# A hybrid decoder block: layer norms on VectorE alone in one row, the output projection's trailing products first, and a first chunk loaded and split by contraction tile

## The chip, the cores and the metric

The kernel runs on one core of a Trainium2 chip. The metric is the device time of one execution, in microseconds (us): three runs gave 1086.43, 1087.6 and 1087.9, median 1087.6. A separate execution was recorded by the hardware profiler; its rows are used below.

## The reference

One decoder layer on x of 256 tokens by 2048 features, all in float32:

```
proj = x @ w_in                        # 2048 x 6160, cut into conv gates b, c, u, and q, k, v, r, z
y_conv = group_rms_norm(b * causal_dwconv3(c * u))
y_gla  = group_rms_norm(gated linear attention of q, k, v, decay from z) * silu(r)
mix = concat(y_conv, y_gla) @ w_out    # 2048 x 2048
x = layer_norm(alpha * x + mix) * ln1_g + ln1_b
ff = square(relu(x @ w_ff_up)) @ w_ff_down   # 2048 x 8192, 8192 x 2048
x = layer_norm(alpha * x + ff) * ln2_g + ln2_b
```

Layer norm here is: mean and variance over the 2048 features of a token, subtract the mean, divide by the square root of variance plus 1e-5, multiply by a gain and add a bias per feature.

## The kernel before

**Tiles.** The 256 tokens are two tiles (t = 0 and t = 1) of 128 partitions. A matrix product runs over the contraction in tiles of 128; two of them (KC = 2) make a *chunk* of weights, 128 partitions by 2 by up to 512 columns. The weights stream once from HBM in chunks, through a pool of 13 raw buffers.

**Three products for one.** Every float32 operand is split into a high part (rounded to the matmul's input type) and a low part, the rest: `split` (L109 to L111) copies the high part on ScalarE (L110) and subtracts on VectorE (L111). `products` (L145) then does three matmuls per contraction tile: high by high (L155), high by low (L156), low by high (L157). So one chunk for one token tile is six matmuls of 512 columns, and each chunk costs one ScalarE copy and one VectorE subtraction of 128 x 1024.

**Who orders the work.** A list scheduler orders the instructions of each engine when the kernel is built: by program order where several are ready, by its own estimate of when they are ready. `tc.issue_after(ins)` sets one instruction behind another in the issue order of the same engine; it adds no wait. `queued(on, ...)` (L100) chains what it emits on one engine in this way while `queue` has a key for that engine: during the first block of the input projection for "pe", "act", "dve" and "sync".

**Lagged products.** `Lagged` (L162) runs a chunk's product for t = 0 at once and puts the one for t = 1 off by `lag` chunks. Each product is a step; `soon` is a list of [count, function]: after each step every count goes down by one, and at zero the function is emitted, with `issue_after` the step's last matmul. Split weights wait in 9 slots (5 "hl" and 4 "s8") from the split to the product for t = 1. In the output projection the lag is 5, so after the last product for t = 0 five products for t = 1 remain (the *trailing products*).

**Layer norm 1.** When all four 512-column blocks of a token tile have been added up (`done_mix`, L610: residual add L613, block statistics L614), `layer_norm` (L575) merges the statistics (L578), `inv_sqrt` (L223) takes the square root on ScalarE (L226), and five VectorE instructions of one element per partition follow (L228 to L233: reciprocal and one Newton step). Then each block is *centred* (subtract the mean, times the gain, L586 on VectorE) and *scaled* (times the inverse deviation, plus the bias, L595 on VectorE). `LN1_HOW = "dppp"` does the centring of the last three blocks in two steps, on ScalarE (L589) and GpSimd (L590). A finished block is transposed on TensorE into x1T by `put` (L218: four transposes into one of two PSUM banks; then L110 and L111 split the result): at once for t = 0, and after 1 + `X1_WAIT` steps for t = 1.

**Up projection.** `up_first` (L662) starts the feed-forward part: chunk for chunk of w_ff_up against x1T, with the trailing products of the output projection run in turn with it, as the lag (`LAGS`: 5, then 8 for two chunks, then 5) lets them go. Each block of x1T feeds two chunks. Later groups mix the up and down projections; there VectorE also forms sums of weight chunks.

**Layer norm 2** comes at the end, in the same function, once per token tile: all on VectorE for t = 0; `LN2_HOW = "qddp"` for t = 1 (first block: centre and scale on ScalarE and GpSimd; fourth block: centre on both). Each block is stored as it is done.

**Start.** The first block of the input projection (412 columns) loads its chunk 0 of weights (`raw_p`, 412 KB) and of the transposed input (`xr`, 256 KB, `x_ahead`, L262) as one DMA each on SP's queue, weights first, splits the weights, then the input.

Of the kernel before, what the change touches and what calls it, by code (L numbers as in the profile page):

```python
# [18 lines left out]
P = 128  # L19
# [23 lines left out]
LAGS = [LAG] * LAG + [LAG + 3] * 2 + [LAG]  # L43
RING = 4096
LN1_HOW = "dppp"
LN2_HOW = "qddp"
X1_WAIT = [2, 4, 6, 8]
# [4 lines left out]
WAIT_UP = 6  # L52
BEHIND = 6
# [8 lines left out]
def hymba_block(ctx, tc, x, x_t, w_in, conv_w, conv_g, w_gate, gate_b, gla_g, w_out,  # L62
# [53 lines left out]

    homes = [[(hlp, "hl")], 0]
# [20 lines left out]
    def weight_chunks(w, kts, at, ncol, name):  # L138


        for i in range(0, len(kts), KC):
            raw = raw_chunk(w, kts[i], at, ncol, f"{name}_{i}")
            yield kts[i:i + KC], *parts_of(raw, ncol, f"{name}_{i}")
# [46 lines left out]
    def project(lagged, w, kts, at, ncol, lhs, done, name, ps=None, first=True, last=True,  # L190
                before=None, lags=None):

        ps = {} if ps is None else ps
        n = len(kts) // KC
        for i, chunk in enumerate(weight_chunks(w, kts, at, ncol, name)):
            if before is not None:
                before(i)

            if lags is not None:
                lagged.lag = lags[i]  # L200
# [22 lines left out]
    def inv_sqrt(pool, ms, eps_t, eps, n, name):  # L223
# [4 lines left out]
        nc.vector.reciprocal(r, s)  # L228
        q = pool.tile([P, n], F32, tag=f"is_q{n}", name=f"q_{name}")
        nc.vector.tensor_mul(q, r, r)  # L230
        nc.vector.scalar_tensor_tensor(q, ms, eps, q, op0=ALU.add, op1=ALU.mult)
        nc.vector.tensor_scalar(q, q, -0.5, 1.5, op0=ALU.mult, op1=ALU.add)
        nc.vector.tensor_mul(r, r, q)  # L233
        return r

# [17 lines left out]
    with ExitStack() as p1:  # L253
# [8 lines left out]
        def x_ahead(i):  # L262
# [3 lines left out]
            split(xT[half][0][:, j:j + KC, :], xT[half][1][:, j:j + KC, :], raw)  # L266

# [63 lines left out]
        block(*qkvz(0), before=x_ahead)  # L331
# [218 lines left out]
    with ExitStack() as p2:  # L550
# [24 lines left out]
        def layer_norm(t, stats, gt, bt, name, done, how="dddd"):  # L575
            y = ys[t]
            mv = sm2.tile([P, 2], F32, tag="mv", name=f"mv_{name}_{t}")
            nc.vector.bn_aggr(mv, stats)  # L578
            rstd = inv_sqrt(sm2, mv[:, 1:2], eps_ln, LN_EPS, 1, f"{name}_{t}")
            shift = sm2.tile([P, 1], F32, tag="shift", name=f"shift_{name}_{t}")  # L580
            if how != "dddd":
                nc.scalar.mul(shift, mv[:, 0:1], -1.0)
            for b, way in enumerate(how):
                cols = slice(b * D // len(how), (b + 1) * D // len(how))
                if way == "d":
                    nc.vector.scalar_tensor_tensor(y[:, cols], y[:, cols], mv[:, 0:1], gt(cols),  # L586
                                                   op0=ALU.subtract, op1=ALU.mult)
                else:
                    nc.scalar.activation(y[:, cols], y[:, cols], AF.Identity, bias=shift)  # L589
                    nc.gpsimd.tensor_mul(y[:, cols], y[:, cols], gt(cols))  # L590
                if way == "q":
                    nc.scalar.activation(y[:, cols], y[:, cols], AF.Copy, scale=rstd)
                    nc.gpsimd.tensor_add(y[:, cols], y[:, cols], bt(cols))
                else:
                    nc.vector.scalar_tensor_tensor(y[:, cols], y[:, cols], rstd, bt(cols),  # L595
                                                   op0=ALU.mult, op1=ALU.add)
                done(b, cols)

# [11 lines left out]
        def done_mix(t, ps, nb):  # L610
# [5 lines left out]
            if left[t] == 0:  # L616
                def done(b, cols):
# [7 lines left out]
                    if t == 0:  # L625
                        go()
                    else:
                        lag.soon.append([1 + X1_WAIT[b], go])
                layer_norm(t, stats1[t], g1, b1, "ln1", done, how=LN1_HOW)

# [31 lines left out]
        def up_first(hT):  # L662

            for i in range(GROUP // NB):
                def done(t, ps, i=i):
                    r = ht.tile([P, NB], F32, tag="relu", name=f"relu_0_{i}_{t}")
                    hidden(r, ps, hT, i, t, f"h0_{i}_{t}", 1 + WAIT_H)
                if i == 1:
                    homes[:] = [[(hlp, "hl")], 0]
                    lag.lag = 0  # L670
                project(lag, w_up, list(range(KT)), i * NB, NB, x1lhs, done, f"up0_{i}",
                        lags=LAGS if i == 0 else None, before=sums_ahead if i == 1 else None)
# [134 lines left out]
        def add(g, t, ps, c0, n):  # L807
# [9 lines left out]
            if left2[t] == 0:  # L817
                def store(b, cols):
                    queue_of = nc.scalar if LN2_HOW[b] == "q" else nc.sync
                    queue_of.dma_start(out[t * P:(t + 1) * P, cols], y[:, cols])  # L820
                layer_norm(t, stats2[t], *gb2, "ln2", store, how=LN2_HOW if t == NT - 1 else "dddd")
# [46 lines left out]

        hTs = [t8_pair("hT_0")]
# [75 lines left out]
```

## Time and profile before

| what | value |
|---|---|
| runs (median of 3) | 1086.43, 1087.6, 1087.9 (1087.6) us |
| the profiled execution's own time | 1086.87 us |
| its span, first to last instruction | 1085.1 us |
| mean granted TensorE clock (1 is 2.4 GHz) | 0.995 |
| busy: TensorE matmul, VectorE, ScalarE, GpSimd | 98%, 82%, 55%, 1% |
| HBM traffic | 201 GB/s over the span |

The profiled execution took 1.77 us more than its span, and lies 0.73 us under the median of the runs. PE is the matmul side of TensorE, PEld its weight loads, DVE is VectorE, ACT ScalarE, POOL GpSimd, SP the queue that issues most DMAs. A matmul's recorded duration overlaps the next one's, so the spacing of starts is what a matmul costs; VectorE's instructions overlap a little in the same way.

### The profile page before, as it was taken

The numbers are of one execution on the slowest core, as the hardware profiler recorded it, in microseconds if no ns is written. First come the engines' busy times: TensorE is split into PE (matmuls) and PEld (weight loads), VectorE is DVE, ScalarE is ACT, GpSimd is POOL, SyncE is SP. The second block draws the span as 40 slices with busy tenths as digits, with TensorE's granted clock in tenths as the row PEclk, the third lists the DMA queues.
The fourth block names the chain that finished last, engine by engine and source line by source line (L and its number), as shares of the span: only waits on it lengthen the run. The fifth ranks groups of instructions, "written<-read, shape, count | busy, mean of one in ns | idle before, by whom it ended". The sixth has DMA issues, their size and how long they took to land.

```text
span 1085.1 us, 13282 instructions
## 1 busy us (share of the span) xinstructions
PE 1062.4 (98%) x4914; PEld 892.2 (82%) x4914; DVE 888.8 (82%) x1003; ACT 594.0 (55%) x685; POOL 15.4 (1%) x18
## 2 busy tenths in 40 slices
PE   9999999999999979999999999999999999999994
PEld 8998888888888868788888888888888888888884
DVE  6545558567656687999999999999999999999667
ACT  6475554435643535666556556556556656556431
POOL 0000000000000020000000000000000000000001
PEclk9999999999999999999999999999999999999997
DMA  9976358676676644257566567567567467368712
GB/s 342 314 245 212 99 180 275 200 232 212 197 294 194 195 174 136 80 205 256 175 211 217 177 209 235 163 203 236 162 201 257 135 207 259 130 203 263 240 57 78
DMA packets 68678, 218.69 MB, mean 202 GB/s; under 512 B 7107, under 2 KB 17363, under 8 KB 68358
## 3 DMA queue, kind: packets, MB, share of 16 engines
q1 hardware_dynamic: 65024, 207.78, 58.2%
q10 hardware_dynamic: 3590, 10.08, 2.7%
q8 instruction: 38, 0.62, 0.2%
q14 instruction: 26, 0.21, 0.1%
HBM read 214.67 MB, written 3.15 MB: 201 GB/s over the span
## 4 chain that ended last, share of the span: by engine, by line
PE 91%; DVE 6%; ACT 1%; DMA 1%; issue 1%; DVEq 0%
PE ps_dn L156 10%; PE ps_dn L157 10%; PE ps_dn L155 10%; PE ps_p L157 3%; PE ps_p L156 3%; PE ps_p L155 3%; PE ps_o L157 2%; PE ps_o L156 2%; PE ps_o L155 2%; PE ps_upa L155 2%; PE ps_upc L155 2%; PE ps_upa L157 2%; PE ps_upa L156 2%; PE ps_upc L156 2%; PE ps_upc L157 2%; PE ps_upd L155 2%
## 5 line engine op out<-in xcount | busy, mean ns | idle before, releaser
L110 ACT CAST hl_up<-raw_r 128x1024 fp32r<-128x1024 f32 x196 | 206.4, 1054 | 129.8 <-PE ps_dn L157 65.7
L111 DVE TENSOR_TENSOR hl_up<-raw_r,hl_up 128x1024 fp32r<-128x1024 f32 x196 | 236.8, 1218 | 9.8 <-ACT hl_up L110 9.3
L110 ACT CAST hl_dn<-raw_dn 128x1024 fp32r<-128x1024 f32 x128 | 134.9, 1054 | 123.6 <-PE ps_dn L157 104.7
L155 PE MATMUL ps_dn<-hl_dn,hT_hi 128*128 128x512 f32 x496 | 193.5, 391 | 0.0
L157 PE MATMUL ps_dn<-hl_dn,hT_lo 128*128 128x512 f32 x496 | 193.1, 389 | 0.0
L156 PE MATMUL ps_dn<-hl_dn,hT_hi 128*128 128x512 f32 x496 | 193.0, 389 | 0.0
L111 DVE TENSOR_TENSOR hl_dn<-raw_dn,hl_dn 128x1024 fp32r<-128x1024 f32 x128 | 156.0, 1219 | 22.5 <-ACT hl_dn L110 21.6
L157 PEld LDWEIGHTS ps_dn<-hl_dn,hT_lo 128*128 128x128 f32 x496 | 93.1, 188 | 19.6
L155 PEld LDWEIGHTS ps_dn<-hl_dn,hT_hi 128*128 128x128 f32 x496 | 93.1, 188 | 19.2
L156 PEld LDWEIGHTS ps_dn<-hl_dn,hT_hi 128*128 128x128 f32 x496 | 93.1, 188 | 19.1
L111 DVE TENSOR_TENSOR hl_p<-raw_p,hl_p 128x824 fp32r<-128x824 f32 (+1 forms) x40 | 40.3, 1017 | 33.1 <-ACT hl_p L110 31.4
L111 DVE TENSOR_TENSOR hl_o<-raw_o,hl_o 128x1024 fp32r<-128x1024 f32 x32 | 38.8, 1223 | 32.8 <-ACT hl_o L110 32.5
L110 ACT CAST hl_o<-raw_o 128x1024 fp32r<-128x1024 f32 x32 | 33.4, 1055 | 45.2 <-PE ps_o L157 38.5
L155 PE MATMUL ps_p<-hl_p,xT_hi 128*128 128x412 f32 (+1 forms) x160 | 56.1, 351 | 0.3 <-ACT xT_hi L110 0.3
L157 PE MATMUL ps_p<-hl_p,xT_lo 128*128 128x412 f32 (+1 forms) x160 | 56.1, 351 | 0.1
L156 PE MATMUL ps_p<-hl_p,xT_hi 128*128 128x412 f32 (+1 forms) x160 | 56.1, 350 | 0.0
L110 ACT CAST hl_p<-raw_p 128x824 fp32r<-128x824 f32 (+1 forms) x40 | 35.1, 885 | 26.9 <-PE ps_p L157 21.3
L155 PE MATMUL ps_upa<-hl_up,x1T_hi 128*128 128x512 f32 x112 | 45.1, 403 | 0.0
L155 PE MATMUL ps_upc<-hl_up,sum_s 128*128 128x512 f32 x112 | 44.3, 396 | 0.0
L157 PE MATMUL ps_upa<-hl_up,x1T_lo 128*128 128x512 f32 x112 | 43.7, 390 | 0.0
L156 PE MATMUL ps_upa<-hl_up,x1T_hi 128*128 128x512 f32 x112 | 43.7, 390 | 0.0
L156 PE MATMUL ps_upc<-hl_up,sum_s 128*128 128x512 f32 x112 | 43.7, 390 | 0.0
(279 smaller groups left out, 2154.6 us busy)
## 6 DMA issues: line engine op xcount, KB each, us to landing
raw_dn<-in_w_ff_down_dram SPq DMA_DIRECT2D x128, 512.0 KB, 4.2
raw_r<-in_w_ff_up_dram SPq DMA_DIRECT2D x112, 512.0 KB, 3.6
raw_o<-in_w_out_dram SPq DMA_DIRECT2D x32, 512.0 KB, 3.5
raw_p<-in_w_in_dram SPq DMA_DIRECT2D x24, 412.0 KB, 5.4
raw_c<-in_w_in_dram SPq DMA_DIRECT2D x16, 512.0 KB, 4.2
raw_u<-in_w_in_dram SPq DMA_DIRECT2D x16, 512.0 KB, 4.3
raw_b<-in_w_in_dram SPq DMA_DIRECT2D x16, 512.0 KB, 4.2
raw_r<-in_w_in_dram SPq DMA_DIRECT2D x16, 512.0 KB, 3.5
```

Source lines behind the costliest of these rows:

```text
L110: queued("act", lambda: nc.scalar.copy(hi, src))
L111: queued("dve", lambda: nc.vector.tensor_sub(lo, src, hi.bitcast(F32)))
L155: nc.tensor.matmul(ps[:, :ncol], ah, whi[:, j, cols], start=f, stop=False, skip_group_check=more)
L156: nc.tensor.matmul(ps[:, :ncol], ah, wlo[:, j, cols], start=False, stop=False, skip_group_check=more)
L157: nc.tensor.matmul(ps[:, :ncol], al, whi[:, j, cols], start=False, stop=e, skip_group_check=more)
```

## The change

1. `layer_norm` does every block on VectorE. Its instructions are chained by `issue_after` in one order: the first block's centring (while ScalarE takes the root), the five small instructions, the first block's scaling, then centre and scale of the second, third and fourth block in turn. ScalarE and GpSimd no longer take part, in layer norm 1 and 2.
2. After the second block's scaling a mark is left in `held`: once `LN1_BUT` (3 for t = 0, 6 for t = 1) more weight chunks have been split, the VectorE part of all later splits is set behind that instruction.
3. `lag.flush()` before `up_first` emits the five trailing products ahead of the up projection. The lag in the first half of the up group is 6 throughout. Both token tiles' transposes now go through `soon`, with waits [6, 7, 9, 11] and [5, 7, 8, 9] steps.
4. The first chunk (`begin`) is loaded and split contraction tile by contraction tile: input half, weight half, input half, weight half, as four DMAs, with a ScalarE copy and a VectorE subtraction for each half. The order within a half is input first.
5. Layer norm 2 stores its blocks on SP's and ScalarE's queue in turn.

```diff
-LAGS = [LAG] * LAG + [LAG + 3] * 2 + [LAG]
+LAG_UP = 6
-LN1_HOW = "dppp"
-LN2_HOW = "qddp"
-X1_WAIT = [2, 4, 6, 8]
+X1_WAIT = [[6, 7, 9, 11], [5, 7, 8, 9]]
+LN1_BUT = [3, 6]
...
     def parts_of(raw, ncol, name):
...
-        split(hl[:, 0, :, :ncol], hl[:, 1, :, :ncol], raw)
+        behind = None
+        for h in held:
+            behind = h[1] if h[0] <= 0 else behind
+            h[0] -= 1
+        with nullcontext() if behind is None else tc.issue_after(behind):
+            split(hl[:, 0, :, :ncol], hl[:, 1, :, :ncol], raw)
...
+    def in_row(steps):
+
+        for i, step in enumerate(steps):
+            with tc.issue_after(nc.cur_bb.bb.instructions[-1]) if i else nullcontext():
+                step()
...
+        def begin(at, ncol):
+
+            raw = rawp.tile([P, KC, NB], F32, tag="raw", name="raw_begin")
+            hl = hlp.tile([P, 2, KC, NB], F32R, tag="hl", name="hl_begin")
+            src = piece(w_in, 0, at, ncol)
+            for j in range(KC):
+                load(xr[0][:, j, :], x_t[0][:, j, :])
+                load(raw[:, j, :ncol], src[:, j, :])
+                split(xT[0][0][:, j, :], xT[0][1][:, j, :], xr[0][:, j, :])
+                split(hl[:, 0, j, :ncol], hl[:, 1, j, :ncol], raw[:, j, :ncol])
+            return hl[:, 0], hl[:, 1]
...
-        block(*qkvz(0), before=x_ahead)
+        at, ncol, done, name = qkvz(0)
+        block(at, ncol, done, name, before=lambda i: i and x_ahead(i), begun=begin(at, ncol))
...
-        def layer_norm(t, stats, gt, bt, name, done, how="dddd"):
+        def layer_norm(t, stats, gt, bt, name, done, but):
...
+            def centre(cols):
+                nc.vector.scalar_tensor_tensor(y[:, cols], y[:, cols], mv[:, 0:1], gt(cols),
+                                               op0=ALU.subtract, op1=ALU.mult)
+
+            rstd = inv_sqrt(sm2, mv[:, 1:2], eps_ln, LN_EPS, 1, f"{name}_{t}",
+                            meanwhile=lambda: centre(blocks[0]))
+            queue["dve"] = nc.cur_bb.bb.instructions[-1]
+            for b, cols in enumerate(blocks):
+                if b:
+                    queued("dve", lambda: centre(cols))
+                queued("dve", lambda: nc.vector.scalar_tensor_tensor(y[:, cols], y[:, cols], rstd, bt(cols),
+                                                                     op0=ALU.mult, op1=ALU.add))
+                if b == 1:
+                    held.append([but, queue["dve"]])
                 done(b, cols)
+            del queue["dve"]
...
-                    if t == 0:
-                        go()
-                    else:
-                        lag.soon.append([1 + X1_WAIT[b], go])
+                    lag.soon.append([X1_WAIT[t][b], go])
...
+                lag.lag = LAG_UP if i == 0 else 0
...
-                    queue_of = nc.scalar if LN2_HOW[b] == "q" else nc.sync
+                    queue_of = nc.scalar if b % 2 else nc.sync
...
+        lag.flush()
         hTs = [t8_pair("hT_0")]
         up_first(hTs[0])
```

## Rows read from the trace of the kernel before

**Rows 1.** The page's first lines: the span, and each engine's busy time, share of the span and instructions.

```profile
span 1085.1 us, 13282 instructions
PE 1062.4 (98%) x4914; PEld 892.2 (82%) x4914; DVE 888.8 (82%) x1003; ACT 594.0 (55%) x685; POOL 15.4 (1%) x18
```

**Rows 2.** The view of waits, of TensorE's matmul side in the stretch from 360 to 430 us: what waited, for whom, us in total, times, longest.

```profile
PE pt_x L218 <- DVE y L595: 2.8, 1, 2.8
PE pt_x L218 <- issue: 1.7, 1, 1.7
PE pt_x L218 <- DVE x1T_lo L111: 0.8, 1, 0.8
PE ps_up L157 <- DVE x1T_lo L111: 0.7, 1, 0.7
```

**Rows 3.** Busy time by stretch: the stretch and its length, then us busy (and instructions) of PE, PEld, DVE, ACT, POOL, then TensorE's granted clock, the DMA engines' busy share and GB/s.

```profile
402.00:410.00 8.00, 8.00 (x44) 6.64 (x44) 3.07 (x5) 1.98 (x4) 0.00 (x0) 1.00 0.28 113
...
520.00:600.00 80.00, 80.00 (x362) 66.20 (x361) 77.90 (x77) 47.33 (x49) 0.00 (x0) 1.00 0.64 210
...
1071.00:1085.00 14.00, 0.08 (x1) 0.00 (x0) 10.56 (x17) 2.44 (x5) 4.27 (x3) 0.59 0.40 150
```

**Rows 4.** Timeline of PE around layer norm 1: start, duration, line, operation, in brackets the idle time before it and what ended it. The first row starts the output projection's product of the last block, third chunk, for t = 1; the second that of the eighth and last chunk.

```profile
372.42 0.39 PE L155 MATMUL ps_o<-hl_o,mixT_conv_hi 128*128 128x512 f32 x1
...
379.22 0.39 PE L155 MATMUL ps_o<-hl_o,mixT_gla_hi 128*128 128x512 f32 x1
382.43 1.32 PE L218 MATMUL pt_x<-ident,y 128*128 128x128 f32 x8 [2.82 <-DVE y L595]
...
401.25 0.50 PE L157 MATMUL ps_up<-hl_up,x1T_lo 128*128 128x512 f32 x1 [0.69 <-DVE x1T_lo L111]
```

**Rows 5.** One piece of the chain of work that ended last, a `put` on PE: start, length.

```profile
402.44 0.44 PE pt_x L218 x4
```

**Rows 6.** Timeline of VectorE around layer norm 1. L613 is the residual add of the last block of t = 0, L614 its statistics, L578 the merge; L231 and L233 are two of the five small instructions; the two last rows are of t = 1.

```profile
373.49 0.68 DVE L613 SCALAR_TENSOR_TENSOR y<-y,ps_o 128x512 f32<-128x512 f32 x1
374.21 0.69 DVE L614 BATCH_NORM_STATS2 st<-y 128x6 f32<-128x512 f32 x1
374.94 0.26 DVE L578 BATCH_NORM_AGGREGATE mv_ln<-st 128x2 f32<-128x24 f32 x1
...
378.14 1.25 DVE L231 SCALAR_TENSOR_TENSOR q_ln<-mv_ln,q_ln 128x1 f32<-128x1 f32 x1
...
379.62 1.00 DVE L233 TENSOR_TENSOR r_ln<-r_ln,q_ln 128x1 f32<-128x1 f32 x1
380.66 3.71 DVE L595 SCALAR_TENSOR_TENSOR y<-y,r_ln,b_ln 128x512 f32<-128x512 f32 x4
...
385.42 1.27 DVE L111 TENSOR_TENSOR x1T_lo<-pt_x,x1T_hi 128x512 fp32r<-128x512 f32 x2
...
393.62 1.21 DVE L111 TENSOR_TENSOR hl_up<-raw_up,hl_up 128x1024 fp32r<-128x1024 f32 x1
394.75 1.24 DVE L231 SCALAR_TENSOR_TENSOR q_ln<-mv_ln,q_ln 128x1 f32<-128x1 f32 x1
```

**Rows 7.** Timeline of GpSimd, from 373 to 402 us.

```profile
377.32 4.51 POOL L590 TENSOR_TENSOR y<-y,g_ln 128x512 f32<-128x512 f32 x3 [375.19 <-ACT y L589]
391.99 5.21 POOL L590 TENSOR_TENSOR y<-y,g_ln 128x512 f32<-128x512 f32 x3 [10.16 <-ACT y L589]
```

**Rows 8.** Timeline of VectorE in layer norm 2: the first two rows are of t = 0, the others of t = 1.

```profile
1067.92 0.15 DVE L230 TENSOR_TENSOR q_ln<-r_ln 128x1 f32<-128x1 f32 x1
...
1070.17 2.74 DVE L595 SCALAR_TENSOR_TENSOR y<-y,r_ln,b_ln 128x512 f32<-128x512 f32 x4
...
1074.07 0.37 DVE L578 BATCH_NORM_AGGREGATE mv_ln<-st 128x2 f32<-128x48 f32 x1
...
1075.87 1.22 DVE L230 TENSOR_TENSOR q_ln<-r_ln 128x1 f32<-128x1 f32 x1
...
1078.34 0.15 DVE L232 TENSOR_SCALAR q_ln<-q_ln 128x1 f32<-128x1 f32 x1
1078.53 0.16 DVE L233 TENSOR_TENSOR r_ln<-r_ln,q_ln 128x1 f32<-128x1 f32 x1
1078.72 3.08 DVE L595 SCALAR_TENSOR_TENSOR y<-y,r_ln,b_ln 128x512 f32<-128x512 f32 x3
```

**Rows 9.** Timeline of the start: three DMA issues on SP's queue (chunk 0 of the weights and of the input, chunk 1 of the weights), two ScalarE copies (chunk 0 and 1), a VectorE subtraction and the matmul that waited for it (both of chunk 1).

```profile
0.80 0.66 SPq L114 DMA_DIRECT2D raw_p<-in_w_in_dram  x1
...
1.52 0.58 SPq L114 DMA_DIRECT2D xr<-in_x_t_dram  x1
...
2.15 0.55 SPq L114 DMA_DIRECT2D raw_p<-in_w_in_dram  x1
...
4.41 0.88 ACT L110 CAST hl_p<-raw_p 128x824 fp32r<-128x824 f32 x1 [2.12 <-DMA raw_p<-in_w_in_dram]
...
6.89 0.88 ACT L110 CAST hl_p<-raw_p 128x824 fp32r<-128x824 f32 x1 [0.98 <-DMA raw_p<-in_w_in_dram]
...
8.74 0.68 DVE L111 TENSOR_TENSOR xT_lo<-xr,xT_hi 128x512 fp32r<-128x512 f32 x1
...
9.48 0.46 PE L157 MATMUL ps_p<-hl_p,xT_lo 128*128 128x412 f32 x1
```

**Rows 10.** Busy time by stretch at the start, columns as in rows 3.

```profile
3.50:4.00 0.50, 0.50 (x4) 0.50 (x4) 0.00 (x0) 0.00 (x0) 0.00 (x0) 1.00 1.06 387
```

More of the change, by code (lines that the diff above doesn't have):

```diff
@@ L114, in load @@
         queued("sync", lambda: nc.sync.dma_start(dst, src))
+    held = []
     homes = [[(hlp, "hl")], 0]
@@ L136, in raw_chunk, with weight_chunks @@
         return raw[:, :, :ncol]
-    def weight_chunks(w, kts, at, ncol, name):
+    def weight_chunks(w, kts, at, ncol, name, begun=None):
         for i in range(0, len(kts), KC):
+            if i == 0 and begun is not None:
+                yield kts[i:i + KC], *begun
+                continue
             raw = raw_chunk(w, kts[i], at, ncol, f"{name}_{i}")
@@ L190, in project @@
     def project(lagged, w, kts, at, ncol, lhs, done, name, ps=None, first=True, last=True,
-                before=None, lags=None):
+                before=None, begun=None):
         ps = {} if ps is None else ps
         n = len(kts) // KC
-        for i, chunk in enumerate(weight_chunks(w, kts, at, ncol, name)):
+        for i, chunk in enumerate(weight_chunks(w, kts, at, ncol, name, begun)):
             if before is not None:
                 before(i)
-            if lags is not None:
-                lagged.lag = lags[i]
             def work(t, i=i, chunk=chunk):
@@ L227, in inv_sqrt @@
         r = pool.tile([P, n], F32, tag=f"is_r{n}", name=f"r_{name}")
-        nc.vector.reciprocal(r, s)
         q = pool.tile([P, n], F32, tag=f"is_q{n}", name=f"q_{name}")
[L230 to L233, printed above, removed]
-        return r
+        steps = [lambda: nc.vector.reciprocal(r, s),
+                 lambda: nc.vector.tensor_mul(q, r, r),
+                 lambda: nc.vector.scalar_tensor_tensor(q, ms, eps, q, op0=ALU.add, op1=ALU.mult),
+                 lambda: nc.vector.tensor_scalar(q, q, -0.5, 1.5, op0=ALU.mult, op1=ALU.add),
+                 lambda: nc.vector.tensor_mul(r, r, q)]
+        if meanwhile is None:
+            for step in steps:
+                step()
+        else:
+            in_row([meanwhile] + steps)
+        return r
+    def in_row(steps):
+        for i, step in enumerate(steps):
+            with tc.issue_after(nc.cur_bb.bb.instructions[-1]) if i else nullcontext():
+                step()
     def row(v, n0, n):
@@ L573, in gains @@
             return rows(g, "g"), rows(b, "b")
-        def layer_norm(t, stats, gt, bt, name, done, how="dddd"):
+        def layer_norm(t, stats, gt, bt, name, done, but):
             y = ys[t]
+            blocks = [slice(b * NB, (b + 1) * NB) for b in range(D // NB)]
             mv = sm2.tile([P, 2], F32, tag="mv", name=f"mv_{name}_{t}")
             nc.vector.bn_aggr(mv, stats)
[L579 to L587, printed above, removed]
-                else:
[L589 to L596, printed above, removed]
@@ L623, in go @@
                         put(y[:, cols], x1T[b // 2], b % 2, t, f"x1_{t}{b}")
[L625 to L629 removed]
+                    lag.soon.append([X1_WAIT[t][b], go])
+                layer_norm(t, stats1[t], g1, b1, "ln1", done, LN1_BUT[t])
         def mix(nb, kts, ps, first, last):
@@ L667, in done @@
                     hidden(r, ps, hT, i, t, f"h0_{i}_{t}", 1 + WAIT_H)
+                lag.lag = LAG_UP if i == 0 else 0
                 if i == 1:
                     homes[:] = [[(hlp, "hl")], 0]
-                    lag.lag = 0
                 project(lag, w_up, list(range(KT)), i * NB, NB, x1lhs, done, f"up0_{i}",
-                        lags=LAGS if i == 0 else None, before=sums_ahead if i == 1 else None)
+                        before=sums_ahead if i == 1 else None)
         KH = KT // 2
```

4 lines of the change are left out of this document (2 added, 2 removed).

## The prediction, made before the run

> **What bounds the kernel now.** I read the page's first lines, then the busy time by stretch, then the waits of TensorE, then timelines of the few places where TensorE waits. The first lines show matmuls busy for 98% of the span and VectorE second with 82% [rows 1]. In the middle of the feed-forward part PE is busy for all 80.00 us of a stretch and VectorE for 77.90 [rows 3]: nothing there can be gained by arranging, and the change leaves it alone. So the end moves only where PE is idle. That is in three places: the start, until the first chunks are split; layer norm 1, where four waits make 2.8 + 1.7 + 0.8 + 0.7 = 6.0 us [rows 2]; and after the last matmul, where PE is busy for 0.08 us of 14 and VectorE for 10.56 [rows 3].
>
> In layer norm 1 the reader is to see that VectorE is the bound, not its share over the kernel: from 373.49, where it takes the residual add of t = 0, it goes from one instruction to the next until PE's last wait ends at 401.25 [rows 4, 6]. The same rows show why it is late. Two of the small instructions on one element take 1.25 and 1.00 us, and four scalings 3.71 [rows 6]; in layer norm 2, without GpSimd beside them, one such small instruction takes 0.15 and four scalings 2.74 [rows 8]. GpSimd's centring runs from 377.32 to 381.83 and from 391.99 to 397.20 [rows 7], and the stretched instructions lie in these spans. I read it as GpSimd holding VectorE up; layer norm 2 of t = 1 repeats it, with 1.22 for one small instruction while GpSimd works and 0.15 after [rows 8].
>
> **Layer norm 1, part by part.** First what VectorE pays per piece. Independent scalings follow each other at 2.74 / 4 = 0.68, with the last one's tail; dependent instructions a little slower: the residual add and its statistics 374.21 - 373.49 = 0.72 [rows 6], dependent small ones 78.53 - 78.34 = 0.19 [rows 8]. A weight split costs 394.75 - 393.62 = 1.13, an x1T split 1.27 / 2 = 0.63 [rows 6].
>
> Removed: the delay by GpSimd. For t = 0: 1.25 - 0.15 + 1.00 - 0.15 + 3.71 - 2.74 = 2.9 us [rows 6, 8]. For t = 1 L231 has 1.24 again [rows 6]; with two more like it I count 3.0. Together 5.9. Added: three centrings per tile, 6 x 0.68 = 4.1; five small instructions in a row at 0.19 instead of between others at about 0.07 (an overlap of 0.15 with what follows), 2 x 5 x 0.12 = 1.2; so VectorE's sum falls by only 0.6 us. The gain has to come from the order, and the order is what changes.
>
> The new order on PE, at rows 4's own pace: five products from 372.42 to 379.22 make 1.36 each, and a `put` 0.44 [rows 5]. Counting steps from the last product of t = 0, the first block's transposes come after the sixth step, at 379.22; then the last trailing product to 381.02, transposes, up chunk 0 from 381.46. With lag 6, seven chunks of t = 0 (9.52) and five more `put`s (2.2) come before the first up product of t = 1, at 393.18.
>
> On VectorE: statistics from 373.49 to 375.2 [rows 6]; then the row: centre 0.7, small ones 0.95, scale 0.7, so block 0 is done at 377.6. Before, the transposes waited for L595 until 382.43, 2.82 us [rows 4]; that wait goes whole, since 377.6 lies ahead of 379.22, and the trailing products are the cover: they last until 381.02. What is late next is VectorE itself. Until the first up product of t = 1 can run whole, at 393.18 + 0.45 without waits, it must do: statistics 1.7, the row of t = 0 (2.35 + 3 x 1.4 = 6.55), statistics and first block of t = 1 (1.7 + 2.35 = 4.05), splits of up chunks 3 to 7 (5 x 1.13 = 5.65; chunks 0 to 2 are split by then), five x1T splits (3.15): 21.1 us from 373.49, so 394.6, a wait of 1.0. That is the best case. The scheduler takes the row of t = 1 as it stands in the program, so two more of its blocks (2 x 1.4) come ahead: 397.4, a wait of 3.8. Both ends are bounds; between them I take 2.5, as x1T splits can be taken between dependent instructions. So PE's waits fall from 6.0 to 2.5 (1.0 to 3.8): **3.5 us gained** (2.2 to 5.0).
>
> The mark in `held` adds an issue order, not a wait: behind it stand the splits of up chunks 3 and later (t = 0) and 6 and later (t = 1), and PE waits for these if they are late. Chunk 3 is wanted at 385.98 + 0.23, and the mark passes at 379.0; the chunk has 7 us for 1.13. The later splits are in the sum above. Where VectorE has no such cover, one split costs PE 1.13. After the region VectorE has room: 3.07 of 8 us busy [rows 3], so nothing is handed on to the next group, and steps of 3 us earlier are paid for there. ScalarE loses six centrings and is not on this path.
>
> **The start.** PE runs without a gap from the matmul at 9.48, which waited for the input split of *chunk 1*, on VectorE from 8.74; its chain began with ScalarE's copy at 6.89, after 0.98 us of waiting for that chunk's DMA [rows 9]. Chunk 0 in halves lets the first matmul begin earlier (the first copy waited until 4.41), but PE then stops for the same chunk 1. So the earlier start is worth nothing. It can cost: two more issues go before chunk 1's load on SP's queue, at (2.15 - 0.80) / 2 = 0.68 each, 1.35 us in all [rows 9]. At most chunk 1 lands 1.35 later, and PE with it. At least nothing: the DMA engines are saturated (387 GB/s, share 1.06) while it waits [rows 10], so it lands when the bytes before it are through, and these are the same. A gain is excluded, as nothing in the change brings chunk 1 forward. I take a loss of 0.2, near the saturated row.
>
> The Trainium skill speaks against this part: SBUF — State Buffer, section "Summary: rules for kernel authors", advises for a DMA-bound transfer all 128 partitions and one DMA, not several. By that rule the start would lose; by the row it loses little, because the queue stays full. The rule's result is a rival below.
>
> **Layer norm 2.** VectorE's work is the chain here. t = 1 now takes 0.37 + 0.73 + 0.95 + 0.7 + 3 x 1.4 = 6.95 from 1074.07, so to 1081.0, where before it ended at 1078.72 + 3.08 = 1081.80 [rows 8]: 0.8 gained. But t = 0 goes the same way, before it on the same engine: it was interleaved without GpSimd, and the row costs it 0.6 for the small instructions and 4 x 0.05 for dependent pairs, 0.8 lost. Sum 0, bounds -0.8 (the statistics of t = 1 fill all gaps of t = 0) and +0.8 (t = 1 gains nothing). The stores change queue, not number, and the last one follows the last scaling as before.
>
> **The sum.** -3.5 + 0.2 + 0 = -3.3 us: the profiled execution's 1086.87 becomes 1083.6. It lies 0.73 under the median of the runs, so for the median I forecast 1087.6 - 3.3 = **1084.3**, its own range from 2.2 - 1.35 - 0.8 (nothing gained) to 5.0 + 0.8: 1081.8 to 1087.6.
>
> **Rivals.** *All four waits go* (chance 0.2): the scheduler, whose estimate no longer misses GpSimd's hold, fills PE with up chunks of t = 0 while t = 1 is normed. For it: the best case above leaves only 1.0. Against: VectorE has no idle time to give. Gain 5 to 6.0, with 0.8 of the tail: 1081.3.
>
> *VectorE's queue gives it back* (0.18): splits and x1T splits get in between dependent steps of both rows, as splits did before (the one at 393.62 stands in the middle of t = 1's small instructions [rows 6]); five of them, 5.65 us, ahead of t = 1's blocks put 5 of the 6 us back. Time 1086.8.
>
> *Several DMAs cost what one would not* (0.12): each issue on SP's queue delays what is behind it in full, so chunk 1 lands 1.35 us later, not 0.2; layer norm's gain stays: 1084.3 + 1.15 = 1085.5. For it: the issues of rows 9 follow one another without a gap. Against: the full queue of rows 10. This is what the Trainium skill's rule, as cited above, comes to.
>
> *GpSimd is not the cause* (0.08), the slower side: the long small instructions wait for something that stays (the neighbours on ScalarE, the order itself). Then VectorE carries 4.1 + 1.2 = 5.3 us more between 373 and 401 and nothing less, and PE waits for it one for one, less the trailing products' cover of 1.8 us: slower by 3.5, 1091.1. It decides from where the removed hold is under the added 5.3. Against it: 0.15 in layer norm 2 without GpSimd [rows 8].
>
> **How the numbers follow.** The forecast has 0.42, the rivals 0.2, 0.18, 0.12 and 0.08. A measurement tells 0.2%, about 2.2 us, from no change: faster is below 1085.4, slower above 1089.8. Faster: 0.38 + 0.2 + 0.05 = 0.63 of them; slower: 0.08 and a little of the rest, 0.1; same 0.27. The range reaches from 1080.9, under the rival without waits, to 1087.5, over the one that gives it back, and leaves out the slower side.
>
> **What would show it.** Right: no GpSimd rows; the small instructions at 0.15 to 0.19; transposes of block 0 right after the seventh chunk's trailing product with no idle time; waits of PE between 376 and 400 of 1 to 4 us in sum, the remaining ones for x1T or weight splits; PE's gapless run starting at 9.5 to 9.9 for chunk 1, with an earlier first matmul; the last scaling 10.0 to 11.5 us after the last matmul. Wrong: a wait of several us for L595 of t = 1; a chunk 1 that lands after 7.3 us; small instructions that still take 1 us; or new waits of PE in the up group, from which the lag of 6 and the nine slots would have to be read again.

## The result, and the profile after

The changed kernel takes 1081.82 us (median of 6 runs, 1081.49 to 1084.46) against 1087.75 us (6 runs, 1086.43 to 1089.2) for the kernel before on the same chip: ratio 0.9949, 95% interval 0.9937 to 0.9962. The forecast was 1084.3, in a range of 1080.9 to 1087.5: the sign was right, and the median lies in the range, but the gain of 5.9 us is nearly twice the 3.3 forecast. The profiled execution took 1082.51 us, 0.69 above the median.

The page's first lines after, against [rows 1]: GpSimd is gone but for constants at the start, VectorE's sum fell by 1.9 us.

```profile
span 1080.8 us, 13265 instructions
...
PE 1062.7 (98%) x4914; PEld 892.4 (83%) x4914; DVE 886.9 (82%) x1014; ACT 588.2 (54%) x675; POOL 1.4 (0%) x9
```

TensorE's waits from 360 to 430 us, against [rows 2]: of 6.0 us, 0.9 are left.

```profile
PE ps_up L167 <- DVE x1T_lo L110: 0.7, 1, 0.7
PE ps_up L165 <- ACT x1T_hi L109: 0.2, 1, 0.2
```

TensorE's timeline, against [rows 4]. The transposes of block 0 stand behind the trailing products without idle time, the 2.82 us before them are gone; the last row is the first up product of t = 1.

```profile
380.33 0.40 PE L167 MATMUL ps_o<-hl_o,mixT_gla_lo 128*128 128x512 f32 x1
380.57 0.60 PE L225 MATMUL pt_x<-ident,y 128*128 128x128 f32 x4
...
384.19 0.50 PE L167 MATMUL ps_up<-hl_up,x1T_lo 128*128 128x512 f32 x1 [0.72 <-DVE x1T_lo L110]
...
394.04 0.50 PE L165 MATMUL ps_up<-hl_up,x1T_hi 128*128 128x512 f32 x1 [0.21 <-ACT x1T_hi L109]
```

VectorE beside it, against [rows 6]: the residual add; two small instructions at 0.16, where there were 1.25 and 1.00; the first x1T split, which the first wait above is for; splits of weights, three of them before 394 and two right behind t = 1's last scaling; and, of t = 1, the first block's scaling, the third block's centring and the first x1T split.

```profile
374.83 0.68 DVE L645 SCALAR_TENSOR_TENSOR y<-y,ps_o 128x512 f32<-128x512 f32 x1
...
377.63 0.16 DVE L239 SCALAR_TENSOR_TENSOR q_ln<-mv_ln,q_ln 128x1 f32<-128x1 f32 x1
...
378.01 0.16 DVE L241 TENSOR_TENSOR r_ln<-r_ln,q_ln 128x1 f32<-128x1 f32 x1
...
380.98 1.22 DVE L110 TENSOR_TENSOR hl_up<-raw_up,hl_up 128x1024 fp32r<-128x1024 f32 x1
...
383.45 0.68 DVE L110 TENSOR_TENSOR x1T_lo<-pt_x,x1T_hi 128x512 fp32r<-128x512 f32 x1
...
386.51 1.21 DVE L110 TENSOR_TENSOR hl_up<-raw_up,hl_up 128x1024 fp32r<-128x1024 f32 x1
...
389.19 1.21 DVE L110 TENSOR_TENSOR hl_up<-raw_up,hl_up 128x1024 fp32r<-128x1024 f32 x1
...
391.82 0.75 DVE L624 SCALAR_TENSOR_TENSOR y<-y,r_ln,b_ln 128x512 f32<-128x512 f32 x1
...
393.93 0.75 DVE L615 SCALAR_TENSOR_TENSOR y<-y,mv_ln,g_ln 128x512 f32<-128x512 f32 x1
394.60 0.68 DVE L110 TENSOR_TENSOR x1T_lo<-pt_x,x1T_hi 128x512 fp32r<-128x512 f32 x1
...
397.12 0.74 DVE L624 SCALAR_TENSOR_TENSOR y<-y,r_ln,b_ln 128x512 f32<-128x512 f32 x1
397.78 2.35 DVE L110 TENSOR_TENSOR hl_up<-raw_up,hl_up 128x1024 fp32r<-128x1024 f32 x2
```

The work put off was done in the room that VectorE had, against [rows 3]: 5.05 us of 8 where there were 3.07, and no wait of TensorE follows from it.

```profile
402.00:410.00 8.00, 8.00 (x38) 6.38 (x37) 5.05 (x8) 4.18 (x6) 0.00 (x0) 1.00 0.48 184
```

To compare all kernels I cut each profiled execution at two instructions that all have: **A** ends with the start of the residual add of the last block of t = 0 (373.49 before [rows 6], 374.83 after), **B** runs from there to the start of the last matmul, **C** from there to the end of the last scaling. Before, that last matmul starts at

```profile
1070.80 0.28 PE L157 MATMUL ps_last<-hl_dn,hT_lo 128*128 128x256 f32 x1
```

and the scalings end at 1078.72 + 3.08 = 1081.80 [rows 8]. After, the two rows are

```profile
1066.67 0.28 PE L167 MATMUL ps_last<-hl_dn,hT_lo 128*128 128x256 f32 x1
```
```profile
1076.69 0.75 DVE L624 SCALAR_TENSOR_TENSOR y<-y,r_ln,b_ln 128x512 f32<-128x512 f32 x1
```

Each ratio is to the kernel before on the same chip; four chips were used for the experiments, and its medians there lie between 1087.69 and 1087.93.

| kernel | median us (runs) | ratio to before, 95% interval | A | B | C |
|---|---|---|---|---|---|
| before | 1087.75 (6) | | 373.49 | 697.31 | 11.00 |
| after | 1081.82 (6) | 0.9949 [0.9937, 0.9962] | 374.83 | 691.84 | 10.77 |
| 1 old start | 1081.46 (5) | 0.9942 [0.9930, 0.9955] | 374.02 | 691.86 | 10.77 |
| 2 before + new start | 1087.97 (11) | 1.0005 [0.9996, 1.0014] | 374.24 | 698.91 | 10.98 |
| 3 before, norms on VectorE | 1080.90 (5) | 0.9937 [0.9924, 0.9951] | 374.35 | 692.45 | 9.63 |
| 4 whole loads, split in halves | 1081.70 (5) | 0.9947 [0.9935, 0.9960] | 373.97 | 691.84 | 10.76 |
| 5 old order of products | 1084.47 (5) | 0.9968 [0.9956, 0.9980] | 374.37 | 694.05 | 10.78 |
| 6 no row | 1081.72 (5) | 0.9943 [0.9930, 0.9956] | 374.03 | 692.66 | 9.64 |
| 7 no mark | 1086.45 (11) | 0.9986 [0.9977, 0.9994] | 374.02 | 695.30 | 10.77 |
| 8 GpSimd back in layer norm 1 | 1089.81 (12) | 1.0020 [1.0011, 1.0028] | 374.21 | 699.63 | 10.77 |
| 9 as 3, layer norm 1 alone | 1082.55 (5) | 0.9950 [0.9936, 0.9964] | 374.76 | 692.36 | 11.01 |
| 10 as 3, GpSimd busy aside | 1088.67 (11) | 1.0007 [0.9998, 1.0016] | 374.14 | 700.30 | 9.64 |
| 11 as 3, trailing products first | 1082.00 (5) | 0.9947 [0.9934, 0.9959] | 373.90 | 693.44 | 9.64 |
| 12 row in layer norm 1 alone, old start | 1080.54 (5) | 0.9932 [0.9918, 0.9945] | 374.05 | 691.82 | 9.64 |

From before to after B falls by 5.47 and C by 0.23. A, by these two profiles, rises by 1.34; the first two experiments ask whether the start really costs that. (My expectations below call it a fact; it is not.) What follows C, to the end of the span, takes 3.30 us before, 3.36 after and 3.27 in run 3, whose stores of layer norm 2 all go to SP's queue: the second queue shows no gain. The profile of 2 is of the slowest of its runs (1089.38), that of 7 of the fastest (1085.22), so their B is not that of their median.

### The profile page after: what moved, and what is told of

Read it like the earlier page. It is cut to its first block, busy times and chain, and to the rows that moved or that the text cites. A ratio compares the mean times of both kernels' runs of the same rounds, so it can differ in the third digit from the quotient of the medians.

```text
span 1080.8 us, 13265 instructions
## 1 busy us (share of the span) xinstructions
PE 1062.7 (98%) x4914; PEld 892.4 (83%) x4914; DVE 886.9 (82%) x1014; ACT 588.2 (54%) x675; POOL 1.4 (0%) x9
## 4 chain that ended last, share of the span: by engine, by line
PE 93%; DVE 5%; ACT 1%; issue 1%; DMA 1%; SPq 0%; DVEq 0%
PE ps_dn L167 10%; PE ps_dn L166 10%; PE ps_dn L165 10%; PE ps_p L167 3%; PE ps_p L165 3%; PE ps_p L166 3%; PE ps_o L165 2%; PE ps_o L167 2%; PE ps_o L166 2%; PE ps_upa L165 2%; PE ps_upc L165 2%; PE ps_upa L167 2%; PE ps_upa L166 2%; PE ps_upc L166 2%; PE ps_upd L165 2%; PE ps_upc L167 2%
## 5 line engine op out<-in xcount | busy, mean ns | idle before, releaser
L165 PEld LDWEIGHTS ps_dn<-hl_dn,hT_hi 128*128 128x128 f32 x496 | 93.1, 188 | 19.2
L165 PE MATMUL ps_p<-hl_p,xT_hi 128*128 128x412 f32 (+1 forms) x156 | 54.7, 351 | 0.7 <-ACT xT_hi L109 0.7
L166 PE MATMUL ps_p<-hl_p,xT_hi 128*128 128x412 f32 (+1 forms) x156 | 54.6, 350 | 0.0
```

What stands on the lines that cost most here:

```text
L165: nc.tensor.matmul(ps[:, :ncol], ah, whi[:, j, cols], start=f, stop=False, skip_group_check=more)
L166: nc.tensor.matmul(ps[:, :ncol], ah, wlo[:, j, cols], start=False, stop=False, skip_group_check=more)
```

## The experiments

**The start: 1, 2 and 4.** The edit of 1 on the changed kernel (2 puts the new lines, with the `begin` that they call, into the kernel before), and that of 4:

```diff
-        block(at, ncol, done, name, before=lambda i: i and x_ahead(i), begun=begin(at, ncol))
+        block(*qkvz(0), before=x_ahead)
```
```diff
+            load(xr[0][:, 0:KC, :], x_t[0])
+            load(raw[:, :, :ncol], src)
             for j in range(KC):
-                load(xr[0][:, j, :], x_t[0][:, j, :])
-                load(raw[:, j, :ncol], src[:, j, :])
```

Old start in the changed kernel: 

> The changed kernel with the start put back: chunk 0 loaded whole (weights first, then input, one DMA each) and split whole. Theory (the halves of chunk 0 arrive slowly, and chunk 1 1.3 us late behind them): the residual add of the last block of t = 0 comes at about 373.5 again instead of 374.83, and the time falls from 1081.8 to 1080.5 (1080.2 to 1080.8). Rival (the earlier first matmul pays for the late chunk 1, and the 1.34 us come from elsewhere in the first 370 us): same time, 1081.8, and the residual add stays at 374.8.

New start in the kernel before: 

> The kernel before with nothing but the new start (chunk 0 in halves). Theory: chunk 1's input lands at about 9.4 instead of before 7.7, and the time is 1.3 us longer than the kernel before, 1089.0 for its 1087.7. Rival (the start alone gains, because the first matmul begins 0.5 us earlier): 0.5 us shorter, 1087.2.

Whole loads: 

> The changed kernel with chunk 0 loaded by two DMAs instead of four (input first, then weights), still split in halves. Theory (what costs the time is that the loads are cut): the DMA engines move over 300 GB/s from 3.5 us again, chunk 1 lands about 1.3 us earlier than in the changed kernel, time 1080.5. Rival (the four copies and four subtractions of the halves hold chunk 1's split up on ScalarE and VectorE): chunk 1 lands early but is split late; time 1081.8.

Measured: 0.36 us less without the new start, 0.22 more with it alone, 0.12 less with whole loads. None of the three is clear of no change: the intervals of 1 and 4 overlap that of the changed kernel, and that of 2 includes 1. So the medians put the new start at 0.2 to 0.4 us, perhaps nothing, and not at 1.3: the five runs of 1 lie above 1080.8, and ten of the eleven of 2 under 1089.0. Both theories of 1 and 2 miss, and so does the rival of 2; the rival of 1 has the time nearly right, but not the residual add at 374.8. What misled me is that the landing of the first DMAs differs from run to run. The matmul of [rows 9] that waited for chunk 1, at 9.48 before, comes after with the new start at

```profile
10.80 0.46 PE L167 MATMUL ps_p<-hl_p,xT_lo 128*128 128x412 f32 x1
```

and in 1, whose start is that of the kernel before to the letter, at

```profile
9.98 0.46 PE L167 MATMUL ps_p<-hl_p,xT_lo 128*128 128x412 f32 x1
```

half a microsecond from 9.48. All profiles with the old start have it between 9.48 and 10.37, all with the new start between 10.01 and 10.80. A over all profiles says the same: 374.83, 374.24, 374.37, 374.03, 374.02, 374.21 with the new start (mean 374.28), 373.49 to 374.76 in seven with the old one (mean 374.10). The profile of before had an early landing, that of after a late one.

One thing the cut loads do in every profile: from 3.5 to 4.0 us the DMA engines move less. After, against [rows 10]; then 1, with the old start:

```profile
3.50:4.00 0.50, 0.50 (x4) 0.50 (x4) 0.43 (x1) 0.23 (x1) 0.00 (x0) 1.00 0.69 159
```
```profile
3.50:4.00 0.50, 0.50 (x4) 0.50 (x4) 0.00 (x0) 0.00 (x0) 0.00 (x0) 1.00 1.09 376
```

It is 156 to 207 GB/s in the six profiles with the new start, 356 to 402 in the seven with the old one, and 282 in 4, less than the 300 that its theory asked for. The matmul of chunk 1 comes at 9.89 in 4, and the time is still that of the rival. What part of the 0.2 to 0.4 is the cut loads and what the cut splits, 0.12 us between 4 and the changed kernel doesn't tell.

**GpSimd: 3, 8, 9 and 10.** The edits, in this order: of 3 (and 9) on the kernel before, of 10 on 3, of 8 on the changed kernel.

```diff
-LN1_HOW = "dppp"
-LN2_HOW = "qddp"
+LN1_HOW = "dddd"
+LN2_HOW = "dddd"
```
```diff
+ASIDE = 320
...
-            if how != "dddd":
+            if name == "ln1":
                 nc.scalar.mul(shift, mv[:, 0:1], -1.0)
+                aside = asidep.tile([P, ASIDE], F32, tag="aside", name=f"aside_{t}")
+                nc.scalar.activation(aside, gt(slice(0, ASIDE)), AF.Identity, bias=shift)
+                for b in range(5):
+                    nc.gpsimd.tensor_mul(aside, aside, gt(slice(0, ASIDE)))
```
```diff
-                if b:
+                if b and name == "ln1":
+                    nc.scalar.activation(y[:, cols], y[:, cols], AF.Identity, bias=shift)
+                    nc.gpsimd.tensor_mul(y[:, cols], y[:, cols], gt(cols))
+                elif b:
                     queued("dve", lambda: centre(cols))
```

9 changes only the first of the two lines of 3.

Both norms on VectorE: 

> The kernel before with both layer norms wholly on VectorE, but without the row, the mark, the trailing products ahead or the new waits. Theory (GpSimd holds VectorE up, and most of the gain is its going): the small instructions take 0.15 to 0.2 us, TensorE's waits in layer norm 1 fall from 6.0 to about 3.5, and the time falls by 2 to 3, to 1085. Rival (the order is the gain): VectorE has 4 us more to do in the region and nothing covers it; waits of 5 to 7 us, time 1087 to 1088.5.

GpSimd back in layer norm 1: 

> The changed kernel with layer norm 1's blocks 2 to 4 centred on ScalarE and GpSimd again, as in the kernel before; all else (row, mark, trailing products ahead, lag 6, new start) as changed. Theory (GpSimd holds VectorE up while it works): the small instructions and scalings beside GpSimd are stretched again, 1.0 to 1.25 us for an instruction on one element; TensorE's waits rise by 2 to 3.5 us and the time is 1084 to 1085.5. Rival (with the new order TensorE has cover enough for GpSimd's hold too): 1082.

Layer norm 1 alone: 

> The kernel before with only layer norm 1 wholly on VectorE; layer norm 2 stays as it was, with ScalarE and GpSimd for part of t = 1. Theory (all of the gain of the run that had both norms on VectorE, 1080.9, is layer norm 1's; the tail is even): 1080.9 to 1081.2. Rival (layer norm 2 gave part of it): 1081.7 or more.

GpSimd busy aside: 

> The kernel before with both norms on VectorE, and in layer norm 1 of each token tile five multiplications of 128 x 320 on GpSimd into a tile that nobody reads (one ScalarE copy of 128 x 320 feeds them). The instruction order of TensorE and VectorE is that of the run without them, and nothing waits for GpSimd. The output is unchanged. Theory (GpSimd at work stretches VectorE's instructions beside it): small instructions beside it take about 1 us again instead of 0.15, scalings are stretched, TensorE's waits rise by 2 to 4 us over 0.9, and the time is 1083 to 1085.5 instead of 1080.9. Rival (the gain came from the shorter chain over three engines and from the new instruction order, not from GpSimd's absence): VectorE's instructions keep their lengths and the time stays at 1080.9.

Measured: 3, two strings of the kernel before and no other line of the change, gives 1080.90, less than the whole change. TensorE's waits in layer norm 1 are 0.9, not the 3.5 that I expected. Its VectorE shows why the scheduler's own order does well: small instructions lie between centrings, so that one costs 0.07 us, from 377.07 to 377.14.

```profile
377.07 0.16 DVE L228 RECIPROCAL r_ln<-s_ln 128x1 f32<-128x1 f32 x1
377.14 0.73 DVE L586 SCALAR_TENSOR_TENSOR y<-y,mv_ln,g_ln 128x512 f32<-128x512 f32 x1
377.79 0.15 DVE L230 TENSOR_TENSOR q_ln<-r_ln 128x1 f32<-128x1 f32 x1
377.86 0.74 DVE L586 SCALAR_TENSOR_TENSOR y<-y,mv_ln,g_ln 128x512 f32<-128x512 f32 x1
```

9 gives 1082.55, the rival's side: layer norm 2 holds 1.65 us of it by the medians, and 1.4 by C (11.01 against 9.63).

10 shows the mechanism. TensorE and VectorE have the instructions of 3, in layer norm 1 in the order of 3, ScalarE has two small ones more per token tile, and nobody waits for GpSimd; yet the time is 1088.67, 7.8 us more. VectorE's timeline while GpSimd multiplies aside (first row of the second fence):

```profile
378.32 0.88 DVE L232 SCALAR_TENSOR_TENSOR q_ln<-mv_ln,q_ln 128x1 f32<-128x1 f32 x1
379.12 0.74 DVE L592 SCALAR_TENSOR_TENSOR y<-y,mv_ln,g_ln 128x512 f32<-128x512 f32 x1
379.78 0.14 DVE L233 TENSOR_SCALAR q_ln<-q_ln 128x1 f32<-128x1 f32 x1
379.85 1.30 DVE L592 SCALAR_TENSOR_TENSOR y<-y,mv_ln,g_ln 128x512 f32<-128x512 f32 x1
381.07 0.82 DVE L234 TENSOR_TENSOR r_ln<-r_ln,q_ln 128x1 f32<-128x1 f32 x1
...
382.95 3.94 DVE L601 SCALAR_TENSOR_TENSOR y<-y,r_ln,b_ln 128x512 f32<-128x512 f32 x4
```
```profile
377.76 7.25 POOL L588 TENSOR_TENSOR aside<-aside,g_ln 128x320 f32<-128x320 f32 x5 [375.64 <-ACT aside L586]
```

Three instructions are longer by 0.73, 0.56 and 0.67 than without GpSimd (0.15, 0.74, 0.15), four scalings by 3.94 - 2.74 = 1.20, two holds: one hold for each of the five multiplications. For t = 1 there are five holds again, 3.20 us together. The Trainium skill (SBUF — State Buffer, section "Summary: rules for kernel authors") says that where a VectorE instruction has two inputs in SBUF and GpSimd reads SBUF, the second one to issue is blocked until the first is done. This trace agrees in kind: instructions with two inputs are held, and the one with one input, L233, keeps its 0.14. But a hold of some 0.6 us is less than half of the 7.25 / 5 = 1.45 us that GpSimd's own record has for one multiplication, and between two holds the centring at 379.12 keeps its 0.74. Whether GpSimd's record includes time in which it is itself held is not shown.

TensorE pays for that, in waits for VectorE of 3.3 and 2.0 us and 0.8 of issue (6.1, where 3 has 0.9):

```profile
PE pt_x L219 <- DVE y L601: 3.3, 2, 2.9
PE ps_up L157 <- DVE hl_up L112: 2.0, 1, 2.0
...
PE pt_x L219 <- issue: 0.8, 1, 0.8
```

That is 5.2 of B's 7.85 over 3; most of the rest is TensorE's clock, which fell twice (last section). 8 says it of the changed kernel: with GpSimd back in layer norm 1 all of the gain is gone, 1089.81, worse than I expected; an instruction on one element takes 1.01 and 1.15 there. But 8 has more in it than the hold: the scalings need what ScalarE and GpSimd make, and VectorE stands still for t = 1's root, which ScalarE takes late:

```profile
391.54 0.17 DVE L237 RECIPROCAL r_ln<-s_ln 128x1 f32<-128x1 f32 x1 [1.57 <-ACT s_ln L234]
```

**The order: 5, 6, 7 and 11.** 5, 6 and 7 take one of three out of the changed kernel: trailing products first, row, mark. 11 puts the first alone, with the lag of 6 and the new waits that belong to it, into 3.

```diff
-X1_WAIT = [[6, 7, 9, 11], [5, 7, 8, 9]]
+X1_WAIT = [3, 5, 7, 9]
...
-                    lag.soon.append([X1_WAIT[t][b], go])
+                    if t == 0:
+                        go()
+                    else:
+                        lag.soon.append([X1_WAIT[b], go])
...
-                lag.lag = LAG_UP if i == 0 else 0
+            if lags is not None:
+                lagged.lag = lags[i]
...
-        lag.flush()
```
```diff
-            rstd = inv_sqrt(sm2, mv[:, 1:2], eps_ln, LN_EPS, 1, f"{name}_{t}",
-                            meanwhile=lambda: centre(blocks[0]))
+            rstd = inv_sqrt(sm2, mv[:, 1:2], eps_ln, LN_EPS, 1, f"{name}_{t}")
...
-                if b:
-                    queued("dve", lambda: centre(cols))
...
+                centre(cols)
...
```
```diff
-                if b == 1:
-                    held.append([but, queue["dve"]])
```

Old order of products: 

> The changed kernel with the old order around the up projection: the trailing products run in turn with the up chunks, lags 5 and 8, transposes of t = 0 at once, of t = 1 after 3, 5, 7 and 9 steps; the row, the mark and the new start stay. Theory (the trailing products cover the norm of t = 0, and that order carries about half of the gain): a wait of some 2 to 3 us before the first transposes returns, and the time is 1083.5 to 1085. Rival (the scheduler finds the cover by itself as soon as VectorE alone does the norm): the same 1081.8.

No row: 

> The changed kernel without the row: the norms' VectorE instructions are not chained, and the scheduler places them; the mark stays on the second block's scaling. Theory (the row keeps splits from getting between dependent instructions, worth about 1 us in layer norm 1 and nothing in layer norm 2): 1082.5 to 1083.5, with TensorE's waits in layer norm 1 at about 2 instead of 0.9. Rival (the row only repeats what the scheduler would do, now that its estimate misses no hold by GpSimd): the same 1081.8 within 0.3.

No mark: 

> The changed kernel without the mark: the VectorE part of weight splits may go ahead of the second block's scaling. Theory (the splits fit in behind the row anyway, because the row is chained): within 0.5 of 1081.8. Rival (the mark is what keeps 1.13 us splits out of the row): two or three splits come ahead in each norm, TensorE waits 2 to 4 us more, 1084 to 1086.

Trailing products first, alone: 

> The kernel before with both norms on VectorE and the new order around the up projection (trailing products first, lag 6, the new waits for the transposes), but no row, no mark and the old start. Theory (trailing products first need the mark, or splits come ahead of the norm, as in the run without the mark): 1083 to 1086, with a wait of over 1.5 us for the first transposes. Rival (only the row makes the mark necessary; unchained, the scheduler lets the norm's instructions through): 1080.5 to 1081.5.

Measured: the three lean on each other. With row and mark but the old order (5) it is 1084.47, as the theory had it, though the wait that it named is not there: TensorE waits 1.7 us in all at up products, for x1T, 0.8 more than after, while B is 2.21 longer; the view of waits doesn't show where the rest goes. With row and trailing products but no mark (7) it is 1086.45, a little over the rival's range. Splits go between the small steps that depend on each other, here two of four:

```profile
377.40 0.16 DVE L237 RECIPROCAL r_ln<-s_ln 128x1 f32<-128x1 f32 x1
377.47 1.21 DVE L110 TENSOR_TENSOR hl_up<-raw_up,hl_up 128x1024 fp32r<-128x1024 f32 x1
378.60 0.15 DVE L238 TENSOR_TENSOR q_ln<-r_ln 128x1 f32<-128x1 f32 x1
378.67 1.21 DVE L110 TENSOR_TENSOR hl_up<-raw_up,hl_up 128x1024 fp32r<-128x1024 f32 x1
```

and TensorE stands still for t = 0's first block:

```profile
383.69 0.66 PE L225 MATMUL pt_x<-ident,y 128*128 128x128 f32 x4 [2.42 <-DVE y L624]
```

The profile of 7 is of its fastest run; six of its eleven, at 1086.4 to 1087.4, have a mean granted clock of 0.991 or 0.992 where the profile has 0.994, so the clock cost these six more than the profile shows.

Without the row (6) it is 1081.72, the same as with it: B is 0.82 longer, C 1.13 shorter. The row helps layer norm 1 and hurts layer norm 2, which my theory missed. The new order alone (11) costs 1.10 us on top of 3 (1082.00), between theory and rival; instead of a wait of over 1.5 us for the first transposes there are 0.4 for these and 1.6 for x1T.

**The sum of what was learnt: 12.** The changed kernel with the old start, and in layer norm 2 the plain loop:

```diff
+            if name == "ln2":
+                rstd = inv_sqrt(sm2, mv[:, 1:2], eps_ln, LN_EPS, 1, f"{name}_{t}")
+                for b, cols in enumerate(blocks):
+                    centre(cols)
+                    nc.vector.scalar_tensor_tensor(y[:, cols], y[:, cols], rstd, bt(cols),
+                                                   op0=ALU.mult, op1=ALU.add)
+                    done(b, cols)
+                return
...
-        block(at, ncol, done, name, before=lambda i: i and x_ahead(i), begun=begin(at, ncol))
+        block(*qkvz(0), before=x_ahead)
```

> The changed kernel with the start put back (chunk 0 whole, weights first) and layer norm 2 on VectorE without the row; layer norm 1 keeps row, mark, trailing products first and the new waits. Theory (the parts add up: from the residual add of t = 0 to the last matmul 691.9 us as in the changed kernel, where layer norm 1 alone on VectorE in the old order took 692.45; from the last matmul to the end of the last scaling 9.63 instead of 10.77, because small instructions lie between centrings again): 1.14 us under the changed kernel with the old start, 1080.3. Rival (layer norm 2's row costs nothing once layer norm 1 is early): 1081.4.

Measured 1080.54 (1080.43 to 1080.73), the fastest of all, 7.4 us under before and 0.2 over the theory, with B and C as expected. The end of its VectorE timeline, against [rows 8]:

```profile
1071.73 0.75 DVE L614 SCALAR_TENSOR_TENSOR y<-y,mv_ln,g_ln 128x512 f32<-128x512 f32 x1
1072.39 0.15 DVE L240 TENSOR_SCALAR q_ln<-q_ln 128x1 f32<-128x1 f32 x1
1072.58 0.16 DVE L241 TENSOR_TENSOR r_ln<-r_ln,q_ln 128x1 f32<-128x1 f32 x1
1072.77 2.74 DVE L621 SCALAR_TENSOR_TENSOR y<-y,r_ln,b_ln 128x512 f32<-128x512 f32 x4
```

## Why the prediction was right, and where it was wrong

**The account that the runs give.** Each step is the difference of two kernels' distances from the kernel before on the same chip. Both norms on VectorE (3): -6.85. Row, mark and trailing products, together and in layer norm 1 alone (from 3 to 12): -0.54, and B says -0.63 (692.45 to 691.82). The row in layer norm 2 (from 12 to 1): +1.10, and C says +1.13 (9.64 to 10.77). The new start (from 1 to the changed kernel): +0.36, not clear of nothing. The steps add up to the measured -5.93 because they are a chain; that B and C give two of them the same size is evidence. So the gain is VectorE alone in the norms; row, mark, order and start together give back 0.9.

**GpSimd holds VectorE up: right.** Run 10 shows it, with 3 beside it, and they rule out the rival in which GpSimd is not the cause (1091.1); 8 agrees.

**Layer norm 1, 3.5 us: the mechanism right, the size wrong; B says 5.47.** The forecast left 2.5 us of waits; the trace has 0.93, under my lower bound. The step that failed is the sum of 21.1 us that VectorE had to do before the first up product of t = 1: "splits of up chunks 3 to 7 (5 x 1.13 = 5.65)". The trace has three there, 380.98, 386.51 and 389.19; the next ones come at 397.78. In the next paragraph I said myself that chunks 6 and later stand behind t = 1's mark, and did not take them out of the sum. Without two of 1.13 it is 18.8, near the 19.2 from 374.83 to TensorE's product at 394.04, which came after 0.21 of waiting. Item by item it fits less well: the fifth x1T split comes only at 394.60, and the two further blocks of t = 1 that made the upper bound did come ahead in part (the third's centring starts at 393.93); but that product needs only the first block, scaled at 391.82 + 0.75, its transposes and ScalarE's half of the split. What came is nearest to my first rival, "All four waits go", at 1081.3, to which I gave 0.2; its 0.8 at the tail didn't come. I had not foreseen the other 0.72, for x1T_lo of t = 0's first block: VectorE takes that split at 383.45, behind a weight split, a scaling and a centring.

**"VectorE's queue gives it back"** (1086.8) is the changed kernel without the mark: 1086.45. I had the mechanism and had not weighed that the mark is there against it.

**The start, 0.2: not contradicted (0.2 to 0.4, or nothing), but its reason fell.** I kept the loss small because the DMA engines would move as much as in [rows 10]; with the cut loads they did not, 159 GB/s for 387. That the loss is small all the same was luck, as far as the runs show. The rival of 1.35 fell too, though the two profiles alone would have said that it held. My sign of being wrong, a chunk 1 that lands after 7.3 us, told nothing: ScalarE's copy of it starts at 7.44 after, and with the old start at 7.39 in 1 and 7.67 in 3.

**Layer norm 2, 0: right in sum (-0.23), by two terms each larger than mine.** VectorE alone gains 11.0 - 9.63 = 1.4; the row gives back 1.14, of which 0.76 lies in t = 1 (1077.44 - 1070.31 = 7.13 from the merge of its statistics to the end, against 1076.43 - 1070.06 = 6.37 in run 3). I had t = 1 gain 0.8 and t = 0 lose it.

**The range.** That the median, 1081.82, lies in 1080.9 to 1087.5 owes something to the rivals, which set these ends: the sum's own range stopped at 1081.8, and reached that only with 0.8 from the tail, of which 0.23 came.

## What to carry to other kernels

Before work is moved between engines, ask what the helper does to the engine beside it: here a helper that nobody waits for cost 7.8 us, and a dummy of about the same size beside an unchanged order showed it in one experiment. An order written by hand has to be tried in parts: here leaving one of three parts out costs 2.6 us (5), nothing (6) or 4.6 us (7), and all three together gain 0.5. And a difference at the start of two single profiles is worth what the same instruction differs by between two kernels with the same start.

## What the runs showed of the hardware

**The price of a hold goes with GpSimd's columns, as far as two widths show.** Five multiplications of 320 columns held VectorE for 0.73 + 0.56 + 0.67 + 1.20 = 3.16 us, 1.98 ns per column; before, three of 512 for 1.25 - 0.15 + 1.00 - 0.15 + 3.71 - 2.74 = 2.92 [rows 6, 8], 1.90 ns per column. An instruction on one element pays as much as one on 512 columns (0.73 and 0.67 in 10, where the centring paid 0.56).

**TensorE's clock falls behind a wait, in some executions.** Run 2 has the waits of the kernel before, 2.82 us for the first transposes, and behind them in windows of 2 us (granted clock third from the right):

```profile
382.00:384.00 2.00, 0.82 (x4) 0.83 (x5) 2.00 (x3) 0.01 (x1) 0.57 (x1) 0.58 0.05 20
384.00:386.00 2.00, 2.00 (x9) 1.81 (x8) 2.00 (x3) 1.17 (x2) 0.00 (x0) 0.50 0.00 0
386.00:388.00 2.00, 2.00 (x6) 1.41 (x6) 2.00 (x4) 0.69 (x1) 0.00 (x0) 0.50 0.26 47
```

0.50 is 1.2 GHz. The kernel before, after the same 2.82 us:

```profile
382.00:390.00 8.00, 6.79 (x36) 5.39 (x37) 7.82 (x12) 3.40 (x5) 0.00 (x0) 1.00 0.21 67
```

B is 698.91 there and 697.31 here, 1.6 us apart. It fell in 7, 8 and 10 too (0.79 over 382 to 390 in each), in 10 once more behind the wait of 2.0 us:

```profile
402.00:404.00 2.00, 2.00 (x7) 1.61 (x7) 2.00 (x5) 0.59 (x1) 0.00 (x0) 0.50 0.79 285
```

It fell nowhere from 366 to 430 us in the kernels whose single waits stay under 1.2 us. So a wait of 2 to 3 us can cost more than its length, and taking it away can give back more than the view of waits shows. In the kernel before, 59 of the 62 runs that stood beside the experiments have a mean granted clock of 0.994 or 0.995, like its profile (0.995), and three 0.993 or less, like run 2's profile (0.993): a fall as long as that of run 2 was rare there. A shorter one these means can't tell.
